# Gate tiles of a hybrid decoder layer computed as pairs, with seven block products in place of eight

## The chip, the cores and the metric

The kernel runs on one core of a Trainium2 chip. The metric is the device time of one execution, in microseconds (us). The core has five engines that run their own queues of instructions in order and wait for each other by semaphores: TensorE (PE in the rows; PEld is its weight load), VectorE (DVE), ScalarE (ACT), GpSimd (POOL) and SyncE (SP), which issues the DMAs here.

## The reference

Two layers work on x, 512 rows by 1024 columns, in float32. One input projection feeds three mixers (latent attention, a gated linear recurrence with a convolution, chunkwise retention), a gate path for each, and three sigmoid merge gates of 1024 channels each:

```python
z = einsum('bsd,de->bse', x, w_in[l])
(q_lat, kv_lat, k_pe, g_mla, lru_u, g_lru, r_q, r_k, r_v, g_ret, merge_logits) = split(z)
y_ret = _retention(r_q, r_k, r_v, ...) * silu(g_ret)
gates = sigmoid(merge_logits + b_merge[l]).reshape(B, S, 3, D_MODEL)
mixed = gates[:, :, 0] * (y_mla @ w_branch[l, 0]) + gates[:, :, 1] * (y_lru @ w_branch[l, 1])
        + gates[:, :, 2] * (y_ret @ w_branch[l, 2])
x = layer_norm(ALPHA * x + mixed @ w_out[l])
```

The merge logits are 3072 columns of the input projection and the retention gate 512, together 3584 of its 6816.

## The kernel before

Activations are kept transposed: `xth` and `xtl` hold x as 8 blocks of 128 channels by 512 rows, split in two float32r parts, a high one (a rounded copy) and a low one (the rest). Each product in float32 is three matmuls (`mm3`, L121): high by high, high by low, low by high. The weights are split the same way when they arrive: `load_w` (L111) has a DMA of 512 KB into `wr` (3 buffers), a cast on ScalarE into `wh` (L108) and a subtraction on VectorE into `wl` (L109), with 4 buffers each; it is given a priority 140 instructions ahead of its place.

A column tile of 128 gate channels (`in_tile`, L280) is 8 channel blocks times 3 matmuls, each with a 128x128 weight block as the stationary operand and 512 rows of x as the moving one, into one PSUM bank (`psmm`, 3 banks). `merge` (L603) takes 8 such tiles a branch: sigmoid on ScalarE (L611), a branch product of 4 x 3 matmuls (`psb`), a product by the gate and, from the second branch on, an addition into `mixed` on VectorE (L619, L620). The order of a layer is: latent projections, recurrence, attention, retention (`ret_in` to `ret_out`), merge of the recurrence, normalization of the retention rows (L629 to L643), merge of attention, the retention gate (`gated_rows`, 4 tiles, each with four transposes `psy`), merge of retention, output projection (`pso`).

In a retention tile, VectorE turns queries and keys (`rope`, L211: shuffle, two products, one addition), and then come transposes of keys (`pskt`), scores (`psrs`), states (`pskv`, VectorE's L574 and L576) and outputs (`por`).

The code is traced in order and a scheduler then orders each engine's queue by priority, with its own idea of durations, and hands out the buffers; a queue runs in the order so fixed.

Of the kernel before, what the change touches and what calls it, by code (L numbers as in the profile page):

```python
# [55 lines left out]
WRAW, WHL, NSLOT = 3, 4, 12  # L56
# [8 lines left out]
OFF = 140  # L65


@with_exitstack
def trunk(ctx, tc, x_in, xt_in, pos, vecs, wg, wt, wrv, wuq, wuk, wuv, wlru, wbr, wout, lng, lnb, dec, rett, out):
# [33 lines left out]
    def raw(t):  # L103
        return t.bitcast(F32)
# [16 lines left out]
    def mm3(ps, lhs, rhs, start, stop):  # L121
        (lh, ll), (rh, rl) = lhs, rhs
        nc.tensor.matmul(ps, lh, rh, start=start, stop=False)  # L123
        nc.tensor.matmul(ps, lh, rl, start=False, stop=False)  # L124
        nc.tensor.matmul(ps, ll, rh, start=False, stop=stop)  # L125
# [18 lines left out]
    def v(l, col, n=1):  # L144
        return vec[:, l * NV + col:l * NV + col + n]
# [133 lines left out]
    def layer(l):  # L279
# [8 lines left out]

        def in_rows(chunks, n, st, ps):
# [28 lines left out]
        def gated_rows(ys, y, tg, gcol=None):  # L318
            for c in range(4):
                sg = sig_gate(tg + c, None if gcol is None else v(l, gcol + c))  # L320
                ps = ps_t.tile([P, S], F32, tag="t", name="psy")
                for st in range(NST):
                    nc.tensor.transpose(ps[:, st * P:(st + 1) * P], y[:, st, c * P:(c + 1) * P], ident)
                gated(ys[c], ps, sg)
# [276 lines left out]
        mixhl = []  # L601

        def merge(b, ys, first, last):  # L603
            mh = None
            for d2 in range(4):
                hi, lo = load_w(wbr[l, b, d2], 1024)
                for j in range(2):
                    d = 2 * d2 + j
                    psg = in_tile(T_ME + b * KD + d)
                    gt = slot("gt")  # L610
                    nc.scalar.activation(gt, psg, AF.Sigmoid, bias=v(l, V_BM + b * KD + d))  # L611
                    ps = PS("psb")
                    for k in range(4):
                        w = slice((j * 4 + k) * P, (j * 4 + k + 1) * P)
                        mm3(ps, (hi[:, w], lo[:, w]), ys[k], k == 0, k == 3)
                    if first:
                        nc.vector.tensor_tensor(out=mixed[d], in0=ps, in1=gt, op=ALU.mult)
                        continue
                    nc.vector.tensor_tensor(out=gt, in0=ps, in1=gt, op=ALU.mult)  # L619
                    nc.vector.tensor_tensor(out=mixed[d], in0=mixed[d], in1=gt, op=ALU.add)  # L620
                    if last:
                        if d % 4 == 0:
                            mh = half("mh", F32R)
                        ml = slot("ml", F32R)
                        split(mh[:, d % 4, :], ml, mixed[d])
                        mixhl.append((mh[:, d % 4, :], ml))

        merge(1, yl, True, False)
        for st in range(NST):  # L629
# [14 lines left out]
        yhi, ylo = half("ymh", F32R), half("yml", F32R)  # L644
        ys = [(yhi[:, c, :], ylo[:, c, :]) for c in range(4)]
        for c in range(4):
            split(ys[c][0], ys[c][1], ym[:, c, :])
        merge(0, ys, False, False)
        ys = pairs("yrp")
        gated_rows(ys, yr, T_GR, V_GN)  # L650
# [138 lines left out]
```

## Time and profile before

| | us |
|---|---|
| median of 3 runs | 1062.96 (1062.69 to 1063.1) |
| the profiled execution | 1063.41 |
| its span, first to last instruction | 1061.4 |
| merge stage, first layer (268 to 486) | 218.0, TensorE busy 218.0 |
| merge stage, second layer (786 to 1004) | 218.0, TensorE busy 218.0 |

The busy share of an engine is the time in which at least one of its instructions was under way. Matmuls overlap, so their listed durations add up to more than the time they took; the distance from one start to the next is what a matmul occupies. PEclk, the granted clock, is a share of 2.4 GHz.

### The profile page before, as it was taken

What the parts mean: (1) busy time and instruction counts of PE and PEld (TensorE: products, weight loads), DVE (VectorE), ACT (ScalarE), POOL (GpSimd) and SP (SyncE); (2) the same over time, 40 slices, a digit from 0 to 9 for tenths busy, and PEclk for the clock granted to TensorE, in tenths of its full rate; (3) what the DMA queues carried; (4) which work ended last, traced back from release to release, by engine and by line L of the source; (5) the groups of instructions that cost most, each with busy time, mean ns of one, the idle gap of its engine ahead of it and who ended that gap; (6) DMA issues with size and microseconds to landing.
All of it is one profiled execution on the core that took longest, in us unless ns stands there. A gap on an engine that the chain in (4) does not pass through costs nothing.

```text
span 1061.4 us, 13791 instructions
## 1 busy us (share of the span) xinstructions
PE 1042.6 (98%) x5260; PEld 875.0 (82%) x5260; DVE 691.9 (65%) x1294; ACT 422.8 (40%) x718; POOL 51.1 (5%) x101
## 2 busy tenths in 40 slices
PE   7999999999999999999999999999999999999997
PEld 6977788888888888888898787888888888888886
DVE  5998989877534435446656889997764353454465
ACT  4549576512323223333123595764123232333320
POOL 1100011000002000000001000110000020000000
PEclk9999999999999999999999999999999999999999
DMA  7432421132132323354143225012312333332421
GB/s 235 139 100 82 130 73 40 44 93 103 60 96 84 119 80 101 98 178 146 59 139 99 70 88 155 31 41 80 93 67 80 103 97 99 100 92 89 176 80 60
DMA packets 31265, 103.45 MB, mean 97 GB/s; under 512 B 3936, under 2 KB 4192, under 8 KB 31200
## 3 DMA queue, kind: packets, MB, share of 16 engines
q1 hardware_dynamic: 31200, 102.58, 30.7%
q8 instruction: 41, 0.67, 0.3%
q14 instruction: 24, 0.20, 0.1%
HBM read 96.28 MB, written 4.19 MB: 95 GB/s over the span
## 4 chain that ended last, share of the span: by engine, by line
PE 80%; DVE 10%; ACT 5%; issue 2%; DMA 1%; POOL 0%; SPq 0%; DVEq 0%; ACTq 0%; POOLq 0%
PE psmm L123 14%; PE psmm L124 14%; PE psmm L125 14%; PE psb L123 4%; PE psb L125 4%; PE psb L124 4%; PE pso L125 3%; PE pso L124 3%; PE pso L123 3%; DVE wl L109 2%; PE pss L478 2%; PE por L587 1%; PE po L516 1%; PE psrs L561 1%; PE psg L125 1%
## 5 line engine op out<-in xcount | busy, mean ns | idle before, releaser
L109 DVE TENSOR_TENSOR wl<-wr,wh 128x1024 fp32r<-128x1024 f32 (+4 forms) x161 | 191.3, 1193 | 198.3 <-ACT wh L108 191.7
L108 ACT CAST wh<-wr 128x1024 fp32r<-128x1024 f32 (+4 forms) x161 | 165.5, 1030 | 386.9 <-PE psmm L124 319.1
L123 PE MATMUL psmm<-xth,wh 128*128 128x512 f32 x768 | 301.3, 392 | 0.0
L124 PE MATMUL psmm<-xtl,wh 128*128 128x512 f32 x768 | 300.1, 391 | 0.0
L125 PE MATMUL psmm<-xth,wl 128*128 128x512 f32 x768 | 299.3, 390 | 0.0
L125 PEld LDWEIGHTS psmm<-xth,wl 128*128 128x128 f32 x768 | 144.2, 188 | 30.0
L123 PEld LDWEIGHTS psmm<-xth,wh 128*128 128x128 f32 x768 | 144.2, 188 | 29.3
L124 PEld LDWEIGHTS psmm<-xtl,wh 128*128 128x128 f32 x768 | 144.3, 188 | 28.9
L123 PE MATMUL psg<-wh,xth 128*128 128x336 f32 x128 | 41.8, 328 | 7.0 <-ACT wh L108 7.0
L478 PE MATMUL pss<-kt,qt 96*128 96x128 f32 (+3 forms) x128 | 42.0, 434 | 0.0
L124 PE MATMUL psg<-wl,xth 128*128 128x336 f32 x128 | 41.6, 326 | 0.2 <-DVE wl L109 0.2
L485 ACT ACTIVATE pr<-pss,nm 128x128 f32<-128x128 f32 (+1 forms) x64 | 34.0, 532 | 19.5 <-DVE nm L480 16.2
L125 PE MATMUL psg<-wh,xtl 128*128 128x336 f32 x128 | 41.3, 324 | 0.1
L123 PE MATMUL psv<-wh,xth 128*128 128x256 f32 x128 | 36.9, 288 | 0.0
L125 PE MATMUL psv<-wh,xtl 128*128 128x256 f32 x128 | 36.2, 283 | 0.0
L124 PE MATMUL psv<-wl,xth 128*128 128x256 f32 x128 | 36.2, 283 | 0.0
L109 DVE TENSOR_TENSOR ptl<-pspt,pth 128x128 fp32r<-128x128 f32 (+1 forms) x96 | 34.7, 372 | 1.3 <-ACT pth L108 0.4
L619 DVE TENSOR_TENSOR gt<-psb,gt 128x512 f32<-128x512 f32 x32 | 22.1, 691 | 20.5 <-PE psb L125 20.5
L108 ACT CAST pth<-pspt 128x128 fp32r<-128x128 f32 (+1 forms) x96 | 31.0, 336 | 6.6 <-DVE ptl L109 4.1
L480 DVE CUSTOM_DVE_ANT_0 pss<-pss,cmask 128x128 f32<-128x128 f32 (+1 forms) x64 | 30.9, 498 | 3.0 <-PE pss L478 2.5
L611 ACT ACTIVATE gt<-psmm,vec 128x512 f32<-128x512 f32 x48 | 32.7, 681 | 0.0
L123 PEld LDWEIGHTS psg<-wh,xth 128*128 128x128 f32 x128 | 24.8, 194 | 7.6 <-ACT wh L108 7.5
(239 smaller groups left out, 1824.1 us busy)
## 6 DMA issues: line engine op xcount, KB each, us to landing
wr<-in_wt SPq DMA_DIRECT2D x96, 512.0 KB, 3.6
wr<-in_wbr SPq DMA_DIRECT2D x24, 512.0 KB, 3.4
wr<-in_wout SPq DMA_DIRECT2D x16, 512.0 KB, 3.4
wr<-in_wrv SPq DMA_DIRECT2D x8, 512.0 KB, 3.7
wr<-in_wg SPq DMA_DIRECT2D x7, 504.0 KB, 4.5
wr<-in_wuq SPq DMA_DIRECT2D x6, 384.0 KB, 3.8
xs<-in_xt SPq DMA_DIRECT2D x8, 256.0 KB, 5.2
xs<-in_x SPq DMA_DIRECT2D x4, 512.0 KB, 6.1
```

Of the source, the lines that this page charges most:

```text
L108: nc.scalar.copy(hi, src)
L109: nc.vector.tensor_tensor(out=lo, in0=src, in1=raw(hi), op=ALU.subtract)
L123: nc.tensor.matmul(ps, lh, rh, start=start, stop=False)
L124: nc.tensor.matmul(ps, lh, rl, start=False, stop=False)
L125: nc.tensor.matmul(ps, ll, rh, start=False, stop=stop)
L478: nc.tensor.matmul(ps[:, :n], qt[h][:96, i * P:n], kt[h][:96, :n], start=True, stop=True)
L480: nc.vector.tensor_tensor_reduce(out=ps[:, :n], in0=ps[:, :n], in1=cmask[:, S - n:], scale=-1.0, scalar=-NEG, op0=ALU.add, op1=ALU.min, ac ...
L485: nc.scalar.activation(pr[:, :n], ps[:, :n], AF.Exp, bias=nm, scale=-1.0, accum_out=rs)
L516: nc.tensor.matmul(po[:, p * 256:(p + 1) * 256], vhl[j // 2][:, j % 2, h, :], pt[j // 2][e][:, j % 2, :], start=j + e == 0, stop=j + e == ...
L561: nc.tensor.matmul(ps[:, n, :], rk[q, c], rq[q, c], start=True, stop=True)
L611: nc.scalar.activation(gt, psg, AF.Sigmoid, bias=v(l, V_BM + b * KD + d))
L619: nc.vector.tensor_tensor(out=gt, in0=ps, in1=gt, op=ALU.mult)
```

## The change

Two column tiles of gates are now computed together. The 1024 channels of x are cut into two halves and its 512 rows into two halves of 256 columns; the pair of weight tiles gives a 2 x 2 matrix of blocks a11, a12 (first tile, the two channel halves), a21, a22 (second tile). The four result blocks come from seven block products (Strassen's product with 15 sums): a11, a12 and a22 and four sums s1 to s4 of weight blocks, by x blocks and four sums of x blocks. A block product is 4 x 3 matmuls of 256 columns (`prod` in `in_pair`). Three accumulators `psx`, `psy1`, `psz` hold the results, and later products are added into the same bank after its value was copied out; VectorE adds three halves.

GpSimd computes the weight sums (four a pair, in the buffers of the raw weights and one slot) and the x sums (`x_sum`, 20 operations a layer, during retention), ScalarE and VectorE split them into high and low parts. `Blocks` hands out split weight blocks of 512 columns (seven of the gates, two of the branch weights a pair), six ahead of their use. Merge gates and the retention gate go through `in_pair`; the normalization of retention rows is spread over the pairs of the first merge. One more buffer of 128x512 is added.

```diff
-WRAW, WHL, NSLOT = 3, 4, 12
+WRAW, WHL, NSLOT = 3, 4, 13
...
+HS = S // 2
+HK = KD // 2
+AHEAD = 6
...
+        tx = [None] * 4
+        def blocks(k, t):
+            return [(xth[:, HK * k + j, HS * t:HS * t + HS], xtl[:, HK * k + j, HS * t:HS * t + HS]) for j in range(HK)]
+        def sums(i):
+            return [(tx[i][:, j, :HS], tx[i][:, j, HS:]) for j in range(HK)]
...
+        def x_sum(i):
+            sraw[i] = [slot("sx").rearrange("p (a b) -> p a b", a=2) for _ in range(2)]
+            for h in range(2):
+                def b(k, t):
+                    o = (slice(None), slice(HK * k + 2 * h, HK * k + 2 * h + 2), slice(HS * t, HS * t + HS))
+                    return raw(xth[o]), raw(xtl[o])
+                o = sraw[i][h]
+                sub = lambda out, a, c, op=ALU.subtract: nc.gpsimd.tensor_tensor(out=out, in0=a, in1=c, op=op)
+                if i in (0, 2):
+                    (ah, al), (ch, cl) = (b(0, 1), b(0, 0)) if i == 0 else (b(1, 1), b(0, 1))
+                    d = slot("sd2").rearrange("p (a b) -> p a b", a=2)
+                    sub(d, al, cl)
+                    sub(o, ah, ch)
+                    sub(o, o, d, ALU.add)
+                else:
+                    ah, al = b(1, 1) if i == 1 else b(1, 0)
+                    sub(o, ah, sraw[0 if i == 1 else 1][h])
+                    sub(o, o, al, ALU.add)
+        def x_sum_split(i, t):
+            tx[i] = t
+            for h in range(2):
+                split(t[:, 2 * h:2 * h + 2, :HS], t[:, 2 * h:2 * h + 2, HS:], sraw[i][h])
...
+                    names = ["a11", "a12", "s1", "s2", "b1", "s3", "b0", "a22", "s4"]
...
+            def load(self, n, t, wb):
+                rs = []
+                for i in range(2):
+                    r = wraw.tile([P, 1024], F32, tag="wr", name="wr")
+                    nc.sync.dma_start(out=r, in_=wt[l, t + i])
+                    rs.append(r)
+                d = {"a11": rs[0][:, :512], "a12": rs[0][:, 512:], "a21": rs[1][:, :512], "a22": rs[1][:, 512:]}
+                d["s1"] = slot("s1")
+                nc.gpsimd.tensor_tensor(out=d["s1"], in0=d["a21"], in1=d["a22"], op=ALU.add)
+                d["s3"] = d["a21"]
+                nc.gpsimd.tensor_tensor(out=d["s3"], in0=d["a11"], in1=d["a21"], op=ALU.subtract)
+                if wb is not None:
+                    r = wraw.tile([P, 1024], F32, tag="wr", name="wr")
+                    nc.sync.dma_start(out=r, in_=wb)
+                    d["b0"], d["b1"] = r[:, :512], r[:, 512:]
+                self.raws[n] = d
...
+            def make(self):
+                n, t, wb, m = self.jobs[self.made]
+                self.made += 1
+                if n not in self.raws:
+                    self.load(n, t, wb)
+                d = self.raws[n]
+                if not self.free:
+                    hi, lo = whl.tile([P, 1024], F32R, tag="wh", name="wh"), whl.tile([P, 1024], F32R, tag="wl", name="wl")
+                    self.free = [(hi[:, :512], lo[:, :512]), (hi[:, 512:], lo[:, 512:])]
+                hl = self.free.pop(0)
+                split(hl[0], hl[1], d[m])
+                if m == "a11":
+                    d["s2"] = d["a11"]
+                    nc.gpsimd.tensor_tensor(out=d["s2"], in0=d["s1"], in1=d["a11"], op=ALU.subtract)
+                if m == "a12":
+                    d["s4"] = d["a12"]
+                    nc.gpsimd.tensor_tensor(out=d["s4"], in0=d["a12"], in1=d["s2"], op=ALU.subtract)
+                self.ready.append(hl)
+            def upto(self, n):
+                while self.made < min(n, len(self.jobs)):
+                    self.make()
...
+            def more(self):
+                self.upto(self.used + AHEAD)
+        def in_pair(bs, out, last, between):
+            def prod(ps, x, start):
+                hi, lo = bs.take()
+                for j in range(HK):
+                    c = slice(j * P, (j + 1) * P)
+                    mm3(ps, (hi[:, c], lo[:, c]), x[j], start and j == 0, j == HK - 1, True)
+            left, right = slice(0, HS), slice(HS, S)
+            x, y, z = (ps_mm.tile([P, S], F32, tag="mm", name=n)[:, :HS] for n in ("psx", "psy1", "psz"))
+            o1, o2 = out
+            prod(x, blocks(0, 0), True)
+            nc.scalar.copy(o1[:, left], x)
+            bs.more()
+            prod(y, blocks(1, 0), True)
+            nc.vector.tensor_tensor(out=o1[:, left], in0=y, in1=o1[:, left], op=ALU.add)
+            bs.more()
+            prod(z, sums(0), True)
+            bs.more()
+            prod(x, sums(1), False)
+            nc.scalar.copy(o1[:, right], x)
+            bs.more()
+            between(1)
+            bs.more()
+            prod(x, sums(2), False)
+            nc.scalar.copy(o2[:, right], x)
+            nc.vector.tensor_tensor(out=o2[:, right], in0=z, in1=o2[:, right], op=ALU.add)
+            bs.more()
+            between(0)
+            bs.more()
+            prod(x, sums(3), False)
+            last(1, left, x)
+            bs.more()
+            prod(z, blocks(1, 1), False)
+            nc.vector.tensor_tensor(out=o1[:, right], in0=z, in1=o1[:, right], op=ALU.add)
+            last(0, None, None)
+            bs.more()
...
-        def gated_rows(ys, y, tg, gcol=None):
...
+        def gated_rows(ys, y, gcol):
...
+                in_pair(bs, cs, keep, turn)
+                for i in (1, 0):
+                    c = 2 * c2 + i
+                    sg = slot("sg")
+                    nc.scalar.activation(sg, cs[i], AF.Sigmoid)
+                    nc.vector.scalar_tensor_tensor(out=sg, in0=cs[i], scalar=v(l, gcol + c), in1=sg, op0=ALU.mult, op1=ALU.mult)
+                    gated(ys[c], pys[i], sg)
...
+        bs = Blocks([(T_ME + b * KD + 2 * d2, wbr[l, b, d2]) for b in (1, 0) for d2 in range(4)]
+                    + [(T_GR + 2 * c, None) for c in range(2)]
+                    + [(T_ME + 2 * KD + 2 * d2, wbr[l, 2, d2]) for d2 in range(4)])
+        x_sum(0)
+        x_sum_split(0, wide("tx", F32R))
...
+            if q == 3:
+                with tc.high_priority(offset=OFF):
+                    bs.upto(AHEAD)
...
+            if q in (2, 3):
+                i = 1 if q == 2 else 3
+                x_sum(i)
+                x_sum_split(i, half("tx", F32R))
+            if q == 4:
+                x_sum(2)
+        x_sum_split(2, wide("tx", F32R))
...
+        def merge(b, ys, first, last, also=None):
             mh = None
             for d2 in range(4):
-                hi, lo = load_w(wbr[l, b, d2], 1024)
-                for j in range(2):
-                    d = 2 * d2 + j
-                    psg = in_tile(T_ME + b * KD + d)
-                    gt = slot("gt")
-                    nc.scalar.activation(gt, psg, AF.Sigmoid, bias=v(l, V_BM + b * KD + d))
-                    ps = PS("psb")
...
+                def gate(i, part, src):
+                    if i == 0:
+                        nc.scalar.activation(gts[0], gts[0], AF.Sigmoid, bias=bias[0])
+                        return
+                    nc.scalar.activation(gts[1][:, part], src, AF.Sigmoid, bias=bias[1])
+                    nc.scalar.activation(gts[1][:, HS:], gts[1][:, HS:], AF.Sigmoid, bias=bias[1])
+                def branch(j):
+                    hi, lo = bs.take()
+                    ps = psb[j] = PS("psb")
                     for k in range(4):
-                        w = slice((j * 4 + k) * P, (j * 4 + k + 1) * P)
+                        w = slice(k * P, (k + 1) * P)
                         mm3(ps, (hi[:, w], lo[:, w]), ys[k], k == 0, k == 3)
+                in_pair(bs, gts, gate, branch)
+                for j in (1, 0):
+                    d, gt, ps = 2 * d2 + j, gts[j], psb[j]
...
-        merge(1, yl, True, False)
-        for st in range(NST):
...
+        merge(1, yl, True, False, norm_rows)
+        merge(0, [(yhl[0][:, c, :], yhl[1][:, c, :]) for c in range(4)], False, False)
         ys = pairs("yrp")
-        gated_rows(ys, yr, T_GR, V_GN)
+        gated_rows(ys, yr, V_GN)
         merge(2, ys, False, True)
```

How the queues changed, at the end of the first layer's retention (the second layer's reads the same). VectorE before, from the rope of the last query tile on (`rsw`, `rt` are the rope's tiles, `sd` scores, `state` the running state, `wl` a low part of weights):

```order
L214 STREAM_SHUFFLE rsw<-psmm 128x512
L217 TENSOR_TENSOR rt<-psmm,cosr 128x512
L215 TENSOR_TENSOR rsw<-rsw,sinr 128x512
L553 TENSOR_TENSOR rt<-pskt,retw 128x384
L218 TENSOR_TENSOR rt<-rt,rsw 128x512
L563 TENSOR_TENSOR sd<-psrs,dmask 128x512 x2
L574 COPY state_107<-pskv 64x64
L109 TENSOR_TENSOR wl<-wr,wh 128x1024
```

VectorE now, from the same shuffle (`s_2678` is a sum of two weight blocks):

```order
L217 STREAM_SHUFFLE rsw<-psmm 128x512
L220 TENSOR_TENSOR rt<-psmm,cosr 128x512
L218 TENSOR_TENSOR rsw<-rsw,sinr 128x512
L112 TENSOR_TENSOR wl<-s_2678,wh 128x512
L112 TENSOR_TENSOR wl<-wr,wh 128x512 x3
L221 TENSOR_TENSOR rt<-rt,rsw 128x512
L711 TENSOR_TENSOR rt<-pskt,retw 128x384
L721 TENSOR_TENSOR sd<-psrs,dmask 128x512 x2
L732 COPY state_107<-pskv 64x64
```

Four splits of gate and branch weights now stand between the rope's products and its last addition; the split of 1024 columns behind the state is gone.

TensorE before, a little later, at the outputs (`por`) of the last two retention tiles:

```order
L587 MATMUL por<-vr,sd 128x64 x2
L584 MATMUL por<-state_107,rt 128x128
L587 MATMUL por<-vr,sd 128x64 x2
L123 MATMUL psb<-yl,wh 128x512
L587 MATMUL por<-vr,sd 128x64
L584 MATMUL por<-state_107,rt 128x128
L587 MATMUL por<-vr,sd 128x64 x2
L123 MATMUL psmm<-xth,wh 128x512
L587 MATMUL por<-vr,sd 128x64
L124 MATMUL psmm<-xtl,wh 128x512
L125 MATMUL psmm<-xth,wl 128x512
```

TensorE now, at the outputs of the same tile:

```order
L745 MATMUL por<-vr,sd 128x64 x2
L126 MATMUL psb<-yl,wh 128x512
L127 MATMUL psb<-yl,wh 128x512
L742 MATMUL por<-state_107,rt 128x128
L745 MATMUL por<-vr,sd 128x64 x2
L128 MATMUL psb<-yl,wl 128x512
L126 MATMUL psb<-yl,wh 128x512
L742 MATMUL por<-state_107,rt 128x128
L745 MATMUL por<-vr,sd 128x64 x2
L127 MATMUL psb<-yl,wh 128x512
L745 MATMUL por<-vr,sd 128x64
L126 MATMUL psx<-xth,wh 128x256
```

Before, 24 matmuls of a gate tile (`psmm`) run on between the outputs; now five of a branch product (`psb`) stand between them and the first block product (`psx`) begins after.

## Rows read from the trace of the kernel before

**Rows 1.** The page, part 1: busy us of each engine, share of the span, instructions.
```profile
PE 1042.6 (98%) x5260; PEld 875.0 (82%) x5260; DVE 691.9 (65%) x1294; ACT 422.8 (40%) x718; POOL 51.1 (5%) x101
```

**Rows 2.** Busy time by stage: stretch, its length, then PE, PEld, DVE, ACT, POOL, clock, DMA.
```profile
206.00:268.00 62.00, 62.00 (x362) 53.19 (x360) 47.61 (x94) 12.25 (x15) 0.00 (x0) 1.00 0.27 86
...
268.00:486.00 218.00, 218.00 (x979) 180.69 (x978) 97.50 (x121) 69.02 (x85) 6.47 (x4) 1.00 0.33 103
```

**Rows 3.** Waits in 268:486: engine and line, whom for; us in total, times, longest.
```profile
ACT wh L108 <- PE psmm L124: 111.4, 28, 6.5
```

**Rows 4.** Timeline of TensorE, gate tile: start, duration, matmul; first and last of 56.
```profile
299.89 0.39 PE L123 MATMUL psmm<-xth,wh 128*128 128x512 f32 x1
...
312.36 0.39 PE L124 MATMUL psmm<-xtl,wh 128*128 128x512 f32 x1
```

**Rows 5.** Timeline of TensorE, last output rows; first and last of 48 matmuls.
```profile
1048.42 0.28 PE L123 MATMUL pso<-wow,mh 128*128 128x256 f32 x1
...
1054.05 0.28 PE L125 MATMUL pso<-wop,ml 128*128 128x256 f32 x1
```

**Rows 6.** The same stretch, weight loads (PEld).
```profile
1048.42 0.19 PEld L124 LDWEIGHTS pso<-wow,mh 128*128 128x128 f32 x1
...
1053.93 0.19 PEld L125 LDWEIGHTS pso<-wop,ml 128*128 128x128 f32 x1
```

**Rows 7.** Groups by line and form, VectorE: count, busy us, mean ns, idle before.
```profile
L109 DVE TENSOR_TENSOR wl<-wr,wh 128x1024 fp32r<-128x1024 f32 x142 | 172.9, 1219 | 193.3 <-ACT wh L108 186.7 <-PE psmm L124 5.7
...
L109 DVE TENSOR_TENSOR ptl<-pspt,pth 128x256 fp32r<-128x256 f32 x64 | 26.1, 416 | 0.4
...
L109 DVE TENSOR_TENSOR ml<-mixed,mh 128x512 fp32r<-128x512 f32 x16 | 11.0, 688 | 5.5 <-ACT mh L108 5.5
...
L311 DVE SCALAR_TENSOR_TENSOR sg<-psmm,vec,sg 128x512 f32<-128x512 f32 x8 | 6.0, 745 | 0.0
```

**Rows 8.** Groups by line and form, ScalarE.
```profile
L108 ACT CAST wh<-wr 128x1024 fp32r<-128x1024 f32 x142 | 149.2, 1052 | 366.2 <-PE psmm L124 319.1 <-PE psb L124 25.7 <-PE psg L125 10.3
...
L108 ACT CAST mh<-mixed 128x512 fp32r<-128x512 f32 x16 | 10.0, 622 | 26.5 <-DVE mixed L620 26.5
...
L471 ACT COPY vr<-psv 128x256 f32<-128x256 f32 x16 | 6.0, 372 | 10.0 <-PE psv L125 9.9
```

**Rows 9.** The page, part 6: DMA issues, count, size, us to landing.
```profile
wr<-in_wt SPq DMA_DIRECT2D x96, 512.0 KB, 3.6
```

**Rows 10.** Groups by line and form, GpSimd.
```profile
L642 POOL TENSOR_TENSOR rv<-vv,mhalf 128x8 f32<-128x8 f32 x8 | 12.9, 1636 | 284.4 <-DVE vv L640 284.4
...
L132 POOL TENSOR_SCALAR_AFFINE_SELECT cmask<-cmask 128x512 f32<-128x512 f32 x1 | 0.6, 612 | 0.0
```

**Rows 11.** Timeline of GpSimd in attention: two casts of one form.
```profile
161.59 0.29 POOL L495 CAST pth<-zeros 128x128 fp32r<-128x128 f32 x1 [3.82 <-ACT vr L471]
...
169.18 1.13 POOL L495 CAST pth<-zeros 128x128 fp32r<-128x128 f32 x1 [3.67 <-DVE ym L523]
```

**Rows 12.** Timeline of VectorE, the same stretch.
```profile
168.94 1.21 DVE L109 TENSOR_TENSOR wl<-wr,wh 128x1024 fp32r<-128x1024 f32 x1
```

**Rows 13.** Timeline of GpSimd in the first merge: two powers.
```profile
336.17 3.24 POOL L642 TENSOR_TENSOR rv<-vv,mhalf 128x8 f32<-128x8 f32 x2 [140.08 <-DVE vv L640]
```

**Rows 14.** Timeline of VectorE, the same stretch.
```profile
337.83 0.69 DVE L643 TENSOR_TENSOR yr<-yr,rv 128x512 f32<-128x512 f32 x1 [1.62 <-POOL rv L642]
```

**Rows 15.** Timeline of TensorE at the end of the first retention stage.
```profile
254.15 0.49 PE L552 MATMUL pskt<-ident,rt 128*128 128x128 f32 x3
...
259.81 1.71 PE L561 MATMUL psrs<-rt 64*128 64x128 f32 x16
```

**Rows 16.** Timeline of VectorE, the same stretch.
```profile
254.36 0.73 DVE L214 STREAM_SHUFFLE rsw<-psmm 128x512 f32<-128x512 f32 x1
...
256.64 0.68 DVE L218 TENSOR_TENSOR rt<-rt,rsw 128x512 f32<-128x512 f32 x1
```

**Rows 17.** Timeline of TensorE: transposes of one retention-gate tile.
```profile
403.25 0.60 PE L323 MATMUL psy<-ident,yr 128*128 128x128 f32 x4
```

More of the change, by code (lines that the diff above doesn't have):

```diff
@@ L119, in load_w, with mm3 @@
         return hi, lo
-    def mm3(ps, lhs, rhs, start, stop):
+    def mm3(ps, lhs, rhs, start, stop, more=False):
         (lh, ll), (rh, rl) = lhs, rhs
-        nc.tensor.matmul(ps, lh, rh, start=start, stop=False)
-        nc.tensor.matmul(ps, lh, rl, start=False, stop=False)
-        nc.tensor.matmul(ps, ll, rh, start=False, stop=stop)
+        nc.tensor.matmul(ps, lh, rh, start=start, stop=False, skip_group_check=more)
+        nc.tensor.matmul(ps, lh, rl, start=False, stop=False, skip_group_check=more)
+        nc.tensor.matmul(ps, ll, rh, start=False, stop=stop, skip_group_check=more)
     ident = cp.tile([P, P], F32, name="ident")
@@ new lines, in x_sum_split, with __init__, take @@
+        def x_sum_split(i, t):
+            tx[i] = t
+            for h in range(2):
+                split(t[:, 2 * h:2 * h + 2, :HS], t[:, 2 * h:2 * h + 2, HS:], sraw[i][h])
+        class Blocks:
+            def __init__(self, jobs):
+                self.jobs = []
+                self.raws = {}
+                for n, (t, wb) in enumerate(jobs):
+                    names = ["a11", "a12", "s1", "s2", "b1", "s3", "b0", "a22", "s4"]
+                    for m in names:
+                        if wb is not None or m[0] != "b":
+                            self.jobs.append((n, t, wb, m))
+                self.used = self.made = 0
+                self.ready = []
+                self.free = []
+            def load(self, n, t, wb):
[35 more added lines that the diff above has]
+                    self.make()
+            def take(self):
+                self.upto(self.used + 1)
+                self.used += 1
+                return self.ready[self.used - 1]
+            def more(self):
+                self.upto(self.used + AHEAD)
@@ L621, in merge, with norm_rows @@
                     if last:
-                        if d % 4 == 0:
-                            mh = half("mh", F32R)
                         ml = slot("ml", F32R)
                         split(mh[:, d % 4, :], ml, mixed[d])
-                        mixhl.append((mh[:, d % 4, :], ml))
-        merge(1, yl, True, False)
-        for st in range(NST):
+                        mixhl[d] = (mh[:, d % 4, :], ml)
+                if also is not None:
+                    also(d2)
+        yhl = []
+        def norm_rows(st):
+            if st == 0:
+                yhl[:] = [half("ymh", F32R), half("yml", F32R)]
+            split(yhl[0][:, st, :], yhl[1][:, st, :], ym[:, st, :])
             y2 = yr[:, st, :]
@@ L643, in layer @@
             nc.vector.tensor_tensor(out=y3, in0=y3, in1=rv.unsqueeze(2).to_broadcast([P, H, 64]), op=ALU.mult)
[L644 to L648, printed above, removed]
+        merge(1, yl, True, False, norm_rows)
+        merge(0, [(yhl[0][:, c, :], yhl[1][:, c, :]) for c in range(4)], False, False)
         ys = pairs("yrp")
-        gated_rows(ys, yr, T_GR, V_GN)
+        gated_rows(ys, yr, V_GN)
         merge(2, ys, False, True)
```

25 lines of the change are left out of this document (18 added, 7 removed).

## Prediction

> **What bounds the kernel now.** I read the busy shares first: TensorE is busy 98% of the span [rows 1]. That alone proves little, so next the table by stage. In the first layer's merge stage (where all gates concerned are computed; the second layer's is alike) TensorE is busy in every microsecond, 218.0 of 218, at granted clock 1.00, while VectorE has 97.5, ScalarE 69.0 and GpSimd 6.5; in the retention stage ahead of it, TensorE has 62.0 of 62 and VectorE 47.6 [rows 2]. The waits say who is early: in the merges ScalarE waits 111.4 us, in 28 waits, for TensorE to free a weight buffer [rows 3]. So a merge lasts as many matmuls as it has times their start-to-start distance. That distance, not the listed duration, is the price.
>
> **The change on TensorE.** Starts from 299.89 to 312.36 are 55 steps of 512 columns, 226.7 ns each [rows 4]; from 1048.42 to 1054.05, 47 steps of 256 columns, 119.8 ns each [rows 5]. A pair of gate tiles was 2 x 24 matmuls of 512 columns, 48 x 0.2267 = 10.88 us. It becomes 7 products x 12 matmuls of 256 columns, 84 x 0.1198 = 10.06 us. An eighth of the columns goes, but half the columns cost 0.1198/0.2267 = 53%, so 7.5% is saved: 0.82 us a pair, 28 pairs (12 merge and 2 retention-gate pairs in each of 2 layers), 22.9 us. Each matmul loads its own stationary operand, 0.19 us, longer than the new distance; in the same place loads also start every 0.12 us, two under way at once [rows 5, 6], so they don't bound.
>
> The Trainium skill (TensorE: Matmul & The Clock Gate, Back-to-back issue gap) gives N/2.4 + 2.5 ns, estimated 215.8 and 109.2 ns here; by it a pair saves 1.19 us and the change 33 us. The trace has 226.7 and 119.8, and the measurement decides.
>
> **VectorE and ScalarE in the merges.** A pair has 9 splits of 512 columns for 3 of 1024. On VectorE 9 x 0.688 - 3 x 1.219 = +2.5 us, and three additions of a 256-column half from PSUM, nearest row 0.416, +1.2 [rows 7]. On ScalarE 9 x 0.622 - 3 x 1.052 = +2.4 us and about four evacuations of 256 columns at 0.372, +1.5 [rows 8]. With 14 pairs a layer: VectorE 97.5 + 52 = 150, ScalarE 69 + 55 = 124, of some 207 us. Both stay covered by TensorE: blocks are split six products ahead, some 8 us, and a DMA lands in 3.6 us [rows 9]. If that lead were gone, each late block would stop TensorE.
>
> **GpSimd.** It gets 4 operations of 128x512 with two SBUF inputs a pair and 20 a layer for the x sums, 152 in all; no such row exists. Bounds: a one-input 128x512 operation took 0.612 us; a 128x128 cast took 0.29, so four times the elements and two inputs are at most 8 x 0.29 = 2.3 us [rows 10, 11]. I take 1.2, four times the cast, the nearest in kind. The Trainium skill (GPSIMD Engine Reference, Elementwise — side-by-side cycle accounting) has 4497 ns for 2048 elements; scaled, an estimate of 1.12 us, which no trace here shows and which would move nothing in the sum.
>
> The engines share something: the cast at 169.18 took 1.13 us instead of 0.29 and ended just after VectorE's split, with two SBUF inputs, from 168.94 to 170.15 [rows 11, 12]. So GpSimd is shut out by such operations. The reverse isn't shown: under two powers on GpSimd from 336.17 to 339.41 an operation of VectorE with two SBUF inputs kept its 0.69 [rows 13, 14]. For VectorE's loss under a long GpSimd operation I keep 0 and the full overlap as bounds and take a small part.
>
> If they exclude each other fully, a merge pair has 11 to 13 such VectorE operations (9 splits, two additions, in the last merge two splits more), 7.6 to 8.9 us, plus 4 x 1.2, at most 13.7, against 10.06 + 24 x 0.2267 = 15.5 us of TensorE. In the first merge, with a split of the attention rows, two operations of the normalization and a power of 1.636 [rows 10], it is 12 x 0.69 + 1.6 + 4.8 = 14.7. It fits.
>
> **Retention to merge, the main cost.** Before, the last query tile ends at 254.15 and TensorE has transposes, scores and outputs until 259.81, when it needs that tile's rope; VectorE finished the rope at 257.3 [rows 15, 16]. Now four weight splits stand ahead of the rope's last addition: 0.2 + 3 x 0.6 + 4 x 0.6 + 0.7 = 5.1 us after the tile's end, against some 4.7 us of TensorE work ahead of the scores, so 0.4 late. Then the state updates stand among two x-sum splits (1.2) and behind GpSimd's sums, which these wait for, while TensorE's filler is few matmuls where before 24 of a gate tile lay between the outputs. I count 1.5 us there and 1 for the port: 3 us a layer. Bounds 0 (the gaps are filled) and 10 (ten sums of 1.2 all in VectorE's way, less 2 that lie idle). Between them I take the end nearer to the queue as ordered: 6 us for both layers.
>
> **Smaller terms.** In a retention-gate pair two products accumulate into the bank that ScalarE is still copying, with no branch product between. After the fourth, eight transposes (2 x 0.60 [rows 17]) cover the 0.372 copy and its latency; after the fifth only four matmuls, 0.48 us, do: 0.4 a pair, 1.6 in all (0 to 4). The second such pair's result needs an addition, sigmoid, gate product and split, 0.416 + 0.62 + 0.745 + 0.69 + 0.62 + 0.69, with VectorE's three of the second tile 5.9 us [rows 7, 8]; TensorE has four products and half a branch, 7.1 us, until it needs it, but three weight splits (2.1) share VectorE: 1 us a layer, 2 in all (0 to 6). Output projection: the last two tiles come together instead of one after the other, about 4 us after the last product; 18 matmuls (4.1 us) don't need them: 0.5 a layer, 1 in all (0 to 4).
>
> **Sum.** -22.9 + 6 + 1.6 + 2 + 1 = -12.3. The profiled execution took 1063.41 (span 1061.4), 0.45 above the median 1062.96, so 1051.1 by it and 1050.7 by the median: 1051.
>
> **Rivals.**
> *A, nearly the full gain.* TensorE has a retention output or a product to run at each seam; only 2 us are lost: 1042.5. For it: VectorE idles 14 of 62 us there before [rows 2]. Against: its queue is in order and splits now stand inside the rope.
> *B, the gain is given back.* A GpSimd operation shuts VectorE out for its whole length: seams 8 us a layer, gate pairs (seven splits, two gate products of 0.745, two splits of the result) 7.7 + 4.8 = 12.5 against 11.0 of TensorE (84 matmuls and eight transposes), 2 x 1.5 a layer of which the lead hides half, 4 elsewhere: 1063.4 - 22.9 + 16 + 3 + 4 = 1063.5. For it: GpSimd's side of it is seen [rows 11, 12]. Against: [rows 13, 14]. The Trainium skill (SBUF — State Buffer, SBUF: two separate sides) says that whichever of the two starts first holds the pair of ports for its whole instruction; by that rule B; the powers' row does not agree.
> *C, slower.* GpSimd with that exclusion becomes the bound of the merges. At 1.8 us an operation: first merge 8.3 + 1.6 + 7.2 = 17.1 against 15.5, 1.6 x 4; gate pairs 14.9 against 11.0, 3.9 x 2; last merge 16.1, 0.6 x 4: 16.6 a layer, 33 us, with seams of 7 a layer: 1063.4 - 22.9 + 33 + 14 = 1087.5. It decides from about 1.5 us: there first merges and gate pairs exceed TensorE by 7 a layer, which with the 10.6 of the other terms eats the gain. For it: the 2.3 bound; against: the cast's row.
> *D, the weight loads bind:* 84 x 0.19 = 16.0 a pair, +5.1, some 1205. Against it: [rows 5, 6].
>
> **Chances.** Forecast (1045 to 1058) 0.50, A 0.20, B 0.16, C 0.13, D 0.01. A measurement here tells 0.2% (2.1 us) from no change. Faster: 0.50 + 0.20 + a third of B and the mild end of C, 0.77; same: most of B, 0.08; slower: the rest, 0.15. The range reaches from A to just past B, 1042.5 to 1066; C at its full price and D stay out. The forecast's own range is 1045 to 1058.
>
> **What would show it.** Right: gate matmuls 256 columns wide at 0.12 us; TensorE idle of some 3 us around each start of the merges, ended by a VectorE rope or state row; nearly none inside the merges; GpSimd's operation near 1.2 us and its total near 230 us on the page (51 + 152 x 1.2). Wrong: TensorE waiting for weight splits inside the merges (B or C), GpSimd above 1.5 us, VectorE splits well above 0.69, or no idle at the seams (A).

## The result: slower, 1110.6 us for 1063.0, and the profile after

The changed kernel takes 1110.56 us (median; 1110.32 to 1114.45), the kernel before, beside it, 1063.03: a ratio of 1.0458 (95% interval 1.0437 to 1.0478). The forecast was 1051, range 1042.5 to 1066. The profiled execution, the longest of its four, took 1114.45, with a span of 1112.4, 51.0 more than the span of before; what is added up from its rows below is some 4 us more than the medians are apart.

The page of the changed kernel, part 1 (busy us, share of the span, instructions), which answers to [rows 1], and under it the span with the mean granted clock:

```profile
PE 1051.9 (95%) x6268; PEld 923.7 (83%) x6268; DVE 853.6 (77%) x1558; ACT 517.4 (47%) x1010; POOL 283.5 (25%) x253
```
```profile
core 0: 1112.4 us, clock 0.977
```

TensorE idles 1112.4 - 1051.9 = 60.5 us where before it idled 18.8: 41.7 more. It is also busy 9.3 us longer, with an eighth of the gate columns gone. The clock explains that sign: (1 - 0.977) x 1112.4 = 25.6 us of full rate are missing, against some 2 in the kernel before (behind its last matmul, where they cost nothing). So there is less work, done partly at half rate, with new holes between.

TensorE's waits (who, for whom; us in total, times, longest); other lines left out:

```profile
PE psx L126 <- ACT gt L419: 14.9, 14, 3.6
PE psx L126 <- ACT cg L414: 13.0, 4, 4.3
PE psrs L719 <- DVE rt L221: 7.3, 2, 3.7
```

The last row is the forecast seam, the place where the retention ends and the merges begin: the scores (psrs) wait for the last query tile's rope. The first two are inside the merges (`gt`) and the retention-gate pairs (`cg`): TensorE waits to write product bank x again until ScalarE has copied it (L414, L419). The forecast had nothing for the merges and 1.6 us for the gate pairs.

The stretch by stages, layer 0, columns as in [rows 2]:

```profile
224.76:259.08 34.32, 34.32 (x207) 29.52 (x206) 29.98 (x51) 6.21 (x11) 18.49 (x13) 1.00 0.05 17
259.08:262.74 3.66, 0.00 (x1) 0.00 (x1) 3.66 (x4) 2.14 (x4) 3.66 (x3) 0.92 0.00 0
262.74:272.40 9.66, 9.66 (x42) 8.88 (x43) 7.41 (x18) 0.00 (x0) 3.56 (x3) 0.50 0.00 0
272.40:306.71 34.31, 33.26 (x226) 29.86 (x225) 27.48 (x47) 16.28 (x31) 11.45 (x8) 1.00 0.39 123
306.71:511.23 204.52, 189.44 (x1288) 175.54 (x1289) 143.91 (x204) 96.71 (x192) 72.77 (x49) 0.97 0.29 98
```

In the second row TensorE has 0.00 busy, at the seam. In the third it works, but the clock is 0.50 (the lower of its levels, 1.2 GHz), for 9.66 us, half of which is lost. In the last, merges and gate pairs, it idles 15.1 of 204.5 us; VectorE is busy 70% and GpSimd 36%, so no engine's sum is full. The loss is in the order of things, not in an amount.

The second layer's seam reads alike: 3.65 us idle (809.08 to 812.73), then 12.91 us at 0.51. The two seams together cost 7.3 us of idle time and, by these rows, 4.8 + 6.3 = 11.1 us of rate.

**Where the wait comes from.** From the second pair of the second merge, while the blocks of the third are made: rows of VectorE, SyncE, GpSimd, ScalarE and TensorE (start, duration, engine, line, operation, idle time before and its releaser):

```profile
361.47 0.68 DVE L112 TENSOR_TENSOR wl<-wr,wh 128x512 fp32r<-128x512 f32 x1
...
362.67 0.68 DVE L112 TENSOR_TENSOR wl<-wr,wh 128x512 fp32r<-128x512 f32 x1
```
```profile
362.18 1.56 SPq L350 DMA_DIRECT2D wr<-in_wt  x2
```
```profile
368.12 1.29 POOL L354 TENSOR_TENSOR s<-wr 128x512 f32<-128x512 f32 x1 [10.76 <-DMA wr<-in_wt]
369.48 1.30 POOL L356 TENSOR_TENSOR wr<-wr 128x512 f32<-128x512 f32 x1
370.86 1.62 POOL L376 TENSOR_TENSOR wr<-s,wr 128x512 f32<-128x512 f32 x1
372.56 1.27 POOL L379 TENSOR_TENSOR wr<-wr 128x512 f32<-128x512 f32 x1
```
```profile
369.44 0.62 ACT L111 CAST wh<-s 128x512 fp32r<-128x512 f32 x1 [2.64 <-POOL s L354]
372.51 0.62 ACT L111 CAST wh<-wr 128x512 fp32r<-128x512 f32 x1 [2.46 <-POOL wr L376]
373.04 0.36 ACT L419 COPY gt<-psx 128x256 f32<-128x256 f32 x1
```
```profile
369.77 0.28 PE L128 MATMUL psx<-tx,wl 128*128 128x256 f32 x1
...
373.46 0.38 PE L126 MATMUL psx<-tx,wh 128*128 128x256 f32 x1 [0.66 <-ACT gt L419]
```

Read it from below. The product that ScalarE must copy out of x is complete just after 369.77, and the copy takes 0.36, but it starts at 373.04: ahead of it in ScalarE's queue stands the cast of the next pair's sum s2, idle 2.46 us for GpSimd (L376). GpSimd itself sat 10.76 us until the transfer of 362.18 landed. And that transfer could not be issued sooner: there are three raw buffers, a pair fills all three, its sums are written back into them, and each is free only when its last split is made. The splits of 361.47 and 362.67 are such last splits of the second pair: the first ends at 362.15, 0.03 before the transfer. "Six blocks ahead" is what the code asks for; the buffers give one pair at a time. From the buffer's release to the cast of s2 (372.51) it is 10.4 us.

**What GpSimd costs beside VectorE.** The changed kernel's groups by line and form (count, busy us, mean ns, idle before), which answer to [rows 7, 10]:

```profile
L112 DVE TENSOR_TENSOR wl<-wr,wh 128x512 fp32r<-128x512 f32 x216 | 177.2, 839 | 65.3 <-ACT wh L111 63.7
L112 DVE TENSOR_TENSOR wl<-s,wh 128x512 fp32r<-128x512 f32 x28 | 37.4, 1335 | 31.7 <-ACT wh L111 28.3
...
L376 POOL TENSOR_TENSOR wr<-s,wr 128x512 f32<-128x512 f32 x28 | 43.9, 1566 | 11.6 <-DVE wl L112 9.5
L354 POOL TENSOR_TENSOR s<-wr 128x512 f32<-128x512 f32 x28 | 38.7, 1384 | 220.6 <-DMA wr<-in_wt 183.4 <-DVE rt L221 17.2 <-DVE wl L112 10.2
```

A weight sum takes 1.38 to 1.57 us, not 1.2. The split of the first sum, which is made while GpSimd computes the next ones, takes 1.34 where 0.69 was counted. The seam shows how, here beside GpSimd's x sums: the four splits that stand ahead of the rope's last addition (three of them in the first row), the addition, then a row of GpSimd:

```profile
256.98 4.04 DVE L112 TENSOR_TENSOR wl<-wr,wh 128x512 fp32r<-128x512 f32 x3
260.94 1.75 DVE L221 TENSOR_TENSOR rt<-rt,rsw 128x512 f32<-128x512 f32 x1
```
```profile
260.42 1.71 POOL L314 TENSOR_TENSOR sd<-xtl 128x512 f32<-128x512 f32 x1
```

The addition, 0.68 in [rows 16], is listed with 1.75 and ends at 262.69, 0.56 after GpSimd's operation (262.13): it waited for nearly all of it. Three such splits take 1.9 undisturbed (0.69 each, started 0.60 apart); with the addition, 3.2 us of the 3.66 at the seam are such lengthening.

### The profile page after: what moved, and what is told of

The parts are those of the page before. It is cut to its first block, busy times and chain, and to the rows that moved or that the text cites. A ratio compares the mean times of both kernels' runs of the same rounds, so it can differ in the third digit from the quotient of the medians.

```text
span 1112.4 us, 16697 instructions
## 1 busy us (share of the span) xinstructions
PE 1051.9 (95%) x6268; PEld 923.7 (83%) x6268; DVE 853.6 (77%) x1558; ACT 517.4 (47%) x1010; POOL 283.5 (25%) x253
## 4 chain that ended last, share of the span: by engine, by line
PE 49%; DVE 19%; issue 11%; POOL 8%; ACT 6%; DMA 6%; SPq 0%; POOLq 0%; DVEq 0%; ACTq 0%
DVE wl L112 6%; PE psmm L126 4%; PE psmm L128 4%; PE psmm L127 4%; DMA wr<-in_wt 3%; PE psx L126 3%; POOL wr L376 2%; PE psx L127 2%; PE psx L128 2%; PE pso L128 2%; PE pso L126 2%; PE pso L127 2%; POOL wr L356 2%; POOL s L354 2%; ACT wh L111 2%
## 5 line engine op out<-in xcount | busy, mean ns | idle before, releaser
L112 DVE TENSOR_TENSOR wl<-wr,wh 128x512 fp32r<-128x512 f32 (+4 forms) x297 | 272.4, 933 | 91.4 <-ACT wh L111 89.7
L111 ACT CAST wh<-wr 128x512 fp32r<-128x512 f32 (+4 forms) x297 | 209.7, 723 | 254.4 <-PE psmm L127 85.1
L126 PE MATMUL psx<-tx,wh 128*128 128x256 f32 x336 | 100.6, 299 | 31.7 <-ACT gt L419 14.9
L126 PE MATMUL psmm<-xth,wh 128*128 128x512 f32 x320 | 125.8, 393 | 0.0
L127 PE MATMUL psmm<-xtl,wh 128*128 128x512 f32 x320 | 125.0, 391 | 0.0
L128 PE MATMUL psmm<-xth,wl 128*128 128x512 f32 x320 | 124.7, 390 | 0.0
L126 PEld LDWEIGHTS psx<-tx,wh 128*128 128x128 f32 x336 | 66.7, 198 | 43.3 <-ACT gt L419 21.6
L127 PE MATMUL psx<-tx,wh 128*128 128x256 f32 x336 | 97.7, 291 | 0.0
L128 PE MATMUL psx<-tx,wl 128*128 128x256 f32 x336 | 97.7, 291 | 0.0
L128 PEld LDWEIGHTS psmm<-xth,wl 128*128 128x128 f32 x320 | 60.1, 188 | 12.6
L127 PEld LDWEIGHTS psmm<-xtl,wh 128*128 128x128 f32 x320 | 60.1, 188 | 11.9
L127 PEld LDWEIGHTS psx<-tx,wh 128*128 128x128 f32 x336 | 66.9, 199 | 1.3
L376 POOL TENSOR_TENSOR wr<-s,wr 128x512 f32<-128x512 f32 x28 | 43.9, 1566 | 11.6 <-DVE wl L112 9.5
L127 PE MATMUL psg<-wl,xth 128*128 128x336 f32 x128 | 41.6, 326 | 0.3 <-DVE wl L112 0.2
```

Source lines behind the costliest of these rows:

```text
L111: nc.scalar.copy(hi, src)
L112: nc.vector.tensor_tensor(out=lo, in0=src, in1=raw(hi), op=ALU.subtract)
L126: nc.tensor.matmul(ps, lh, rh, start=start, stop=False, skip_group_check=more)
L127: nc.tensor.matmul(ps, lh, rl, start=False, stop=False, skip_group_check=more)
L128: nc.tensor.matmul(ps, ll, rh, start=False, stop=stop, skip_group_check=more)
L376: nc.gpsimd.tensor_tensor(out=d["s2"], in0=d["s1"], in1=d["a11"], op=ALU.subtract)
```

## The experiments

All are edits of the changed kernel unless said otherwise; ratios are to the kernel before on the same chip.

**1. The copies first.** ScalarE's order alone: each cast of a weight block is pinned behind the copy of a product bank that the code has before it.

```
+ copies.append(nc.scalar.copy(o2[:, right], x))        # and the two others
...
+ c = split(hl[0], hl[1], d[m])                         # split returns its cast
+ if copies: order c behind copies[-1]
```

> Only ScalarE's order differs from the changed kernel: each cast of a weight block now stands behind the copies of product banks that the code has before it. Theory Q (queue): TensorE's 31 us of idle time in the merges and gate pairs of both layers come from the copy of an accumulated bank standing behind a cast that waits for a GpSimd sum; they go, and with them most of the 12 us that the lower clock right after them costs: about 1070 us (1065 to 1080). Theory W (weights): the blocks themselves come too late, since a pair's transfers, four sums and splits are one chain behind the previous pair's last splits; then TensorE waits for the weights where it waited for the copy, and at most a third is regained: 1095 to 1110. The two idle stretches of 3.7 us at the retention's end stay under both.

Measured 1131.5 us (ratio 1.0628, 1.0602 to 1.0654): outside both expectations. Q as stated is wrong. The trace shows why; ScalarE, and TensorE's longest wait there:

```profile
329.56 0.62 ACT L111 CAST wh<-s 128x512 fp32r<-128x512 f32 x1 [5.18 <-POOL s L360]
332.60 0.62 ACT L111 CAST wh<-wr 128x512 fp32r<-128x512 f32 x1 [2.42 <-POOL wr L384]
333.13 0.50 ACT L798 ACTIVATE gt<-gt,vec 128x256 f32<-128x256 f32 x1
333.54 1.12 ACT L111 CAST wh<-wr 128x512 fp32r<-128x512 f32 x2
334.57 0.46 ACT L797 ACTIVATE gt<-psx,vec 128x256 f32<-128x256 f32 x1
```
```profile
335.08 0.58 PE L127 MATMUL psy<-xth,wh 128*128 128x256 f32 x1 [4.06 <-ACT gt L797]
```

The copies are nearly in time (waits on them: 7.0 us in all, 1.4 at most), and the same two casts, waiting for the same GpSimd sums, now hold up the activation that empties x at the pair's end. Whatever stands next in that queue pays. So the order alone is not the cause. Why this order is 21 us worse, and not just as bad, the run doesn't separate.

**2. No weight sums.** The four sums of a pair are left out and plain blocks are split in their place, so that the result is no longer the reference's; splits, matmuls, transfers and x sums stay.

```
- nc.gpsimd.tensor_tensor(out=d["s1"], ...)             # s1, s3, s2, s4
+ d["s1"] = d["s3"] = d["a21"]; d["s2"] = d["a11"]; d["s4"] = d["a12"]
```

> The four sums of weight blocks of each pair are left out: the splits take plain blocks in their place (112 GpSimd operations less; the result is then not the reference's); x sums, splits, matmuls and transfers stay. Q and W both: nothing on ScalarE waits for GpSimd in the merges, so their 31 us of idle time and its clock loss go, and what is left is the retention's end: 1066 us (1060 to 1075). If the transfers alone (one pair's three raw buffers) were the bound (theory R), the waits would stay, ended by transfers: above 1090.

Measured 1045.8 us (0.9839, 0.9824 to 0.9854), better than expected: 64.8 us hang on 112 GpSimd operations. Its page and one group:

```profile
PE 1024.8 (98%) x6268; PEld 906.2 (87%) x6268; DVE 792.9 (76%) x1558; ACT 521.3 (50%) x1010; POOL 121.3 (12%) x141
```
```profile
L112 DVE TENSOR_TENSOR wl<-wr,wh 128x512 fp32r<-128x512 f32 x244 | 162.1, 687 | 105.5 <-ACT wh L111 103.9
```

TensorE idles 1043.7 - 1024.8 = 18.9 us, as before the change, and is 17.8 us less busy than in [rows 1]. Spans: 68.7 between the two, 41.6 of idle time and 27.1 of busy time, which the clock (0.977 for 0.999 here) nearly accounts for. R falls: transfers with three buffers do keep up when nothing follows them but a split. But the edit did not touch the merges alone. With the sums gone the scheduler orders VectorE's queue at the seam in another way: no split stands between the rope's products and its last addition, and TensorE doesn't wait there. So the 64.8 us hold the seams too, some 18 us by the rows above.

**3. Weight sums on VectorE.** `nc.gpsimd` becomes `nc.vector` in the four lines.

> The same four sums a pair, on VectorE in place of GpSimd: by the trace an operation of this kind takes 0.68 us there when GpSimd is idle, for 1.38 to 1.57 on GpSimd, and no longer doubles VectorE's operations beside it. Theory X (exclusion: GpSimd's operations cost by shutting VectorE out): VectorE gains 2.8 us of work a pair but loses about as much stretching, the chain of four sums shortens from 5.9 to 2.8 us, and the copies wait less: 1075 us (1065 to 1085). If VectorE is then itself too full (28 of 40 us busy in the merges, theory V), the idle time stays or grows: 1100 or more.

Measured 1068.4 us (1.0052, 1.0037 to 1.0067), as X said; V falls. TensorE's largest wait:

```profile
PE psrs L719 <- DVE rt L221: 14.2, 2, 7.1
```

No other row over 1.6 us concerns the retention or the merges. The buffers and transfers are as in the changed kernel, so its lead is enough when the four sums take 0.68 us each and GpSimd does not lengthen them. What is left is the seam: VectorE's queue there, with sums, splits and GpSimd's x sums beside it, makes the rope 7.1 us late in each layer, and the clock is 0.983 over the run.

**4. The sums, but nobody waits.** Experiment 2, with the four GpSimd operations put back on the raw blocks, into a buffer that nothing reads.

> The run without weight sums, with the four GpSimd operations of each pair put back on the same blocks at the same places, but into a buffer that nothing reads: GpSimd's work beside VectorE is that of the changed kernel, and no split waits for it (the splits take plain blocks, so the result is not the reference's). Theory X (GpSimd's operations cost by shutting VectorE out while they run): nearly all of the 65 us between the changed kernel and the run without sums comes back: 1095 to 1115 us. Theory L (what costs is that splits, and through ScalarE's and VectorE's queues TensorE's banks, wait for a chain of four GpSimd operations behind a late transfer): VectorE's operations are as long as in the changed kernel, but covered by TensorE: 1046 to 1056 us, with some of it at the retention's end.

Measured 1063.8 us (1.0002, 0.9993 to 1.0012): between the two expectations. The split of experiment 2's row:

```profile
L112 DVE TENSOR_TENSOR wl<-wr,wh 128x512 fp32r<-128x512 f32 x244 | 234.2, 985 | 55.9 <-ACT wh L111 55.1
```

985 ns for 687: 72 us more on VectorE for these splits, and the kernel is 18 us longer. So of the 64.8 us, 18 are GpSimd in VectorE's way, and 47 come only when splits must wait for the sums. These 47 are not the merges' alone: at the seam VectorE's queue is that of experiment 2, with the rope's last addition right behind its products,

```profile
257.98 0.68 DVE L221 TENSOR_TENSOR rt<-rt,rsw 128x512 f32<-128x512 f32 x1
```

and TensorE idles 0.93 us there in each layer (before states, not scores), for 3.66 and 3.65. Against the changed kernel some 15 us of the 47 are the seams, by idle time and clock; some 30 are left for the merges and gate pairs. The low clock came here too, behind those 0.93 us:

```profile
258.40:261.70 3.30, 3.30 (x18) 3.30 (x17) 2.24 (x6) 0.00 (x0) 2.96 (x3) 0.50 0.03 5
```

**5. Early transfers for three pairs.** In the second merge, three pairs of each layer take their gate blocks into four buffers that are free by then.

```
+ if n in (5, 6, 7):
+     r = tmp.tile([P, 1024], F32, tag="pair", name="wrp", bufs=4)
+ else:
      r = wraw.tile([P, 1024], F32, tag="wr", name="wr")
```

> The changed kernel, but in the second merge three of the four pairs of each layer take the raw blocks of their gate tiles into the buffers of the first branch's rows, which are free by then, so that their transfers need not wait for the pair before to be split. Theory T (the chain is late because the transfer waits for a raw buffer that the pair before holds to its last splits): GpSimd's sums of these pairs start some 5 us sooner, ScalarE's copies no longer stand behind a cast that waits, and TensorE's idle times at these pairs (in the changed kernel 1.12 and 0.78 us in layer 0, 1.20 and 0.54 in layer 1) and at the first gate pair behind (2.9 us each, with the low clock after it) go: 1110.5 - 9.6 - 3 = 1098 us (1095 to 1103). Theory G (the four GpSimd operations are too long by themselves, whenever they start): no change there, 1108 to 1112.

Measured 1092.8 us (1.0289, 1.0256 to 1.0321; four runs from 1089.5 to 1096.6): below both ranges, on T's side. GpSimd's first two sums for the third pair, and s2:

```profile
354.67 1.74 POOL L357 TENSOR_TENSOR s<-wrp 128x512 f32<-128x512 f32 x1
356.48 1.62 POOL L359 TENSOR_TENSOR wrp<-wrp 128x512 f32<-128x512 f32 x1
...
364.27 1.60 POOL L379 TENSOR_TENSOR wrp<-s,wrp 128x512 f32<-128x512 f32 x1 [6.17 <-DVE wl L112]
```

The operations are as long as ever, but the first starts at 354.67 instead of 368.12, no transfer holds it, and s2 waits for the first block's split, not the other way round. TensorE's waits on the copies in the second merge (3.0 us in layer 0, 342 to 412) are gone. So the late transfer is what made the chain late. Over the run TensorE idles 1089.4 - 1039.0 = 50.4 us, 10.1 less than in the changed kernel, close to T's 9.6. The rest of the gain is not all the edit's: at the seam, where it changed nothing, TensorE waits as long as ever, but the clock stays low for 3.4 us, not 9.66:

```profile
PE psrs L722 <- DVE rt L221: 7.3, 2, 3.6
```
```profile
264.12:267.53 3.41, 3.41 (x18) 3.08 (x19) 2.18 (x6) 0.00 (x0) 2.53 (x3) 0.50 0.00 0
```

Both seams together lose 3.4 us of rate here, for 11.1: 7.7 of the 23.0 us between the two profiled spans.

**6. Pauses in the kernel before.** Four in one merge of each layer: VectorE copies a branch product several times, and a transpose that needs the copy stands before the next tile's matmuls.

```
+ for _ in range(n): nc.vector.tensor_scalar(out=g, in0=g, scalar1=1.0, ...)   # n = 5, 1
+ behind.append(nc.tensor.transpose(pt[:, 0, :], g[:, :P], ident))
```

> The kernel before, with four pauses of TensorE in the merge of the second branch of each layer: after the branch product of a tile VectorE makes a chain of copies and a transpose waits for it, about 3.6 us in layer 0 and 1.3 us in layer 1; the first matmul behind stands in order behind the transpose. Theory C (clock): after a pause of some 3.6 us the granted clock is 0.5 for a stretch of 3.4 us or more, as after the idle stretches of 2.9 to 4.3 us of the changed kernel, and after those of 1.3 us it stays 1.0: 1063 + 4 x (3.6 + 1.7) + 4 x 1.3 = 1089 us. Without it (the low clock has another cause): 1063 + 4 x 3.6 + 4 x 1.3 = 1083 us.

Measured 1076.5 us (1.0126, 1.0106 to 1.0146). The pauses did not come out as planned: TensorE waited at three of eight, 9.0 us in all, so the expected totals can't be compared; two of them can be read by stretch:

```profile
399.14:404.53 5.39, 0.00 (x1) 0.03 (x1) 4.29 (x8) 1.44 (x2) 0.00 (x0) 0.92 0.34 97
404.53:410.48 5.95, 5.95 (x15) 4.69 (x16) 0.00 (x0) 0.00 (x0) 0.00 (x0) 0.50 0.00 0
...
931.23:934.17 2.94, 0.00 (x0) 0.03 (x1) 2.90 (x5) 0.85 (x1) 0.00 (x0) 1.00 0.59 177
934.17:940.00 5.83, 5.83 (x27) 4.82 (x28) 0.45 (x1) 0.25 (x1) 0.00 (x0) 1.00 0.32 93
```

An idle stretch of 5.39 us, put into a kernel whose clock is otherwise 1.00, is followed by 5.95 us at 0.50 (15 matmuls where 27 go otherwise); one of 2.94 us is not. So an idle stretch can bring the clock down by itself. Its length alone does not decide it: behind these 2.94 us the clock stayed, behind the 0.93 us of experiment 4 it fell. What does decide it, these cases don't tell.

**7. The seam in another order.** Experiment 3, and at the retention's end only two blocks are split before the rope; the pair's sums (now all four at once) and further splits, and the last x sums on GpSimd, stand behind the last tile's masks.

```
- bs.upto(AHEAD)                # while the last query tile is computed
+ bs.upto(2)                    # there; upto(AHEAD) follows its scores
+ each later sum and split: order behind the last mask (masked[3])
```

> Weight sums on VectorE, and at the retention's end in another order: before the last query tile's rope only the first two blocks are split, the first pair's sums and further splits stand behind the last tile's masks on VectorE, and the last x sums on GpSimd wait for these masks. By the run with sums on VectorE, TensorE then idles only at the two retention ends (7.1 us each) and loses some 10 us to the clock there; theory S (VectorE's queue at the retention's end holds those sums, splits and GpSimd's lock before the rope): both go, 1043 to 1050 us, faster than the kernel before (1063) and near the run without sums (1046). If the work only moves behind the masks and stops the first products there: 1055 to 1068.

Measured 1058.9 us (0.9968, 0.9956 to 0.9981): 0.3% faster than the kernel before, but the work only moved, as the second alternative said. VectorE, GpSimd and TensorE there:

```profile
271.50 3.43 DVE L112 TENSOR_TENSOR wl<-wr,wh 128x512 fp32r<-128x512 f32 x2
```
```profile
270.99 1.71 POOL L315 TENSOR_TENSOR sx<-xth 128x512 f32<-128x512 f32 x1
```
```profile
273.30 0.58 PE L128 MATMUL psx<-tx,wl 128*128 128x256 f32 x1 [3.09 <-DVE wl L112]
```

Splits of 1.7 us beside GpSimd's x sums stop the fourth product.

**8. The x sums early.** Experiment 7, with these x sums right behind the ones before them and without their extra buffers.

```
- d = slot("sd2"); sub(d, al, cl); sub(o, ah, ch); sub(o, o, d, ALU.add)
+ sub(o, ah, ch); sub(o, o, al, ALU.add); sub(o, o, cl)
- if q == 4: x_sum(2)
+ if q == 3: x_sum(2)           # no longer behind the masks
```

> As the run with VectorE's sums behind the masks, and the last x sums are computed on GpSimd right behind those before them, ahead of the last query tile's rope and without second buffers, so that GpSimd is idle when VectorE makes the first pair's sums and splits. By theory S with GpSimd's lock (the 3.1 us idle at the first pair's fourth block and the low clock after it come from splits of 1.7 us beside these x sums): 1058.9 - 6.2 - 5 = 1047 us (1044 to 1053). If VectorE's queue behind the masks is too long even with operations of 0.68 us, the idle time stays: 1055 to 1060. If the rope becomes late under the earlier x sums: above 1060.

Measured 1048.6 us (0.9864, 0.9849 to 0.9878), as expected, and 14.5 us faster than the kernel before, with all of the change's block products and sums:

```profile
PE 1025.6 (98%) x6268; PEld 905.1 (86%) x6268; DVE 856.8 (82%) x1670; ACT 520.6 (50%) x1010; POOL 119.0 (11%) x141
```
```profile
L112 DVE TENSOR_TENSOR wl<-wr,wh 128x512 fp32r<-128x512 f32 x216 | 142.4, 686 | 20.5 <-ACT wh L111 19.3
```

TensorE is busy within 0.8 us of the run without sums, splits are back at 0.69, the mean clock is 0.998.

## Why the prediction was wrong, step by step

**The matmuls: right in kind, a little small.** 256-column matmuls go at 0.12 us, and without the weight sums TensorE is 17.8 us less busy; 22.9 was forecast. Where the other 5 us stay was not traced. The Trainium skill's formula for the gap of an isolated matmul (TensorE: Matmul & The Clock Gate, Back-to-back issue gap), by which 33 us would have come, is further off.

**The failed step: "Both stay covered by TensorE: blocks are split six products ahead, some 8 us, and a DMA lands in 3.6 us."** VectorE's and ScalarE's sums were rightly below TensorE's, and the step concluded that they are covered. It took the lead from the code and did not ask what a transfer waits for. Three raw buffers hold one pair, so the next pair's chain (buffer free, transfer, four GpSimd sums in a row, 5.8 us by their means, casts in ScalarE's queue) begins when the lead is nearly used up: 10.4 us in the rows above, against a lead of some 8. The step even said what would follow if the lead were gone; it gave that no price. Worth: some 30 of the 64.8 us, what experiments 2 and 4 leave beside GpSimd's 18 and the seams' 15; seen to begin at the transfer by experiment 5. A late transfer alone is covered (experiment 2), and so is one with four sums of 0.68 us behind it (experiment 3); with sums of 1.38 to 1.57 us behind it the lead is gone.

**GpSimd beside VectorE: the small part was too small.** The forecast kept "0 and the full overlap as bounds" and leaned on the powers [rows 13, 14], an operation of 8 columns, against the cast [rows 11, 12]; the cast was the one to trust. By experiment 4 it costs 18 us, although VectorE is busy only 82% there. The Trainium skill's rule (SBUF — State Buffer, SBUF: two separate sides) is that whichever starts first holds the shared ports for its whole instruction; the rope's row above agrees.

**The seam: the idle time right by luck, the clock not in the sum.** 3 us a layer were forecast; measured 3.66 and 3.65. But the three parts were 0.4 for the rope, 1.5 for the state updates and 1 for GpSimd's port; what came is all at the rope, 3.2 of it GpSimd's lengthening, and no wait on a state. (The 1.5 leaned on 24 gate matmuls between the outputs before; 13 lay there, 265.05 to 269.93.) And the 9.66 us at 0.50 behind it lose another 4.8 in layer 0, 6.3 in layer 1. No term of the forecast and no rival had a clock other than 1.00, since the profile of before shows none while TensorE works; 25.6 us of rate are missing in the run. That an idle stretch can cause it is shown for one long pause (experiment 6); experiment 8, with the stretches gone and a clock of 0.998, agrees. Which of the shorter ones do, and for how long, is open.

**The gate pairs.** 0.4 us a pair was counted for the copy after the fifth product; the one after the fourth (L414) was called covered by eight transposes. The four waits are on that one and have 13.0 us, since casts that wait stand ahead of it, as in the merges.

**The rivals.** C had the side right (slower, chance 0.13) but another cause: it took GpSimd as the bound by its sum, with 1.8 us an operation; it is 1.4 to 1.6, and busy 25% of the span. B's exclusion was there as one part of three. That experiment 4 ended at 1063.8 where B said 1063.5 is chance: B put 16 us at the seams, where that run idles 0.93 a layer. With both doubts open about the same new user of GpSimd, 0.15 for slower was too little.

## What to carry to other kernels

A lead is what the buffers allow: for each block follow the buffer's release, the transfer, every operation that derives something, and the in-order queue it ends in, and add up the latencies, not only each engine's busy time. What waits in a queue holds up whatever is behind it, so reordering that queue moves the wait and doesn't end it. Taking work out can let the scheduler reorder a queue elsewhere, so compare the orders before the whole gain is put down to the work. When TensorE gains short idle stretches, price the lower clock behind them too; and an addition put on an idle GpSimd can cost more than the same on a busy VectorE, whose operations with two SBUF inputs it holds up.

## What was not expected of the hardware

After an idle stretch of 3.66 us TensorE ran at 0.50 of its clock for 9.66 us: more was lost behind the hole than in it. In experiment 5 the same stretch was followed by 3.4 us. The Trainium skill (TensorE: Matmul & The Clock Gate, Part 1: The HAM clock gate) has the lower rate of 1.2 GHz after idling; the rows agree in the level. And VectorE's split of 128x512 went from 687 to 985 ns on average when GpSimd added blocks beside it, with nothing waiting for the sums.
